# A hybrid decoder block on one core: expert stage with 2048-wide weight splits, rows out of PSUM by VectorE, pinned column transposes and slots dealt over all partitions

## The chip, the cores and the metric

The kernel runs on one core of a Trainium2 chip. Its time is the device time of one execution in microseconds; the figure given is the median of several executions. The trace is of one more execution, taken by the hardware profiler. Engines are named as in the profile: PE is TensorE (PEld its weight loads), DVE is VectorE, ACT is ScalarE, POOL is GpSimd, SP issues most DMAs.

## The reference

One block of a decoder on 1024 tokens of 2048 features, all in float32. The part that matters here is the last: a mixture of 32 experts. Every token takes the best of four groups of experts and the best two of the eight experts in it.

```python
def expert_block(args):
    xb, e = args
    a = jax.nn.silu(xb @ w_gate[e]) * (xb @ w_up[e])   # 2048 -> 512, twice
    return a @ w_down[e]                                # 512 -> 2048
...
out = zeros.at[slot_tok].add(ys * slot_gate[:, None])   # a token's two rows are summed
x = x + gt2[:, None, :] * out
return rmsnorm(x, g_final)
```

In front of it stand a pooling mixer, sparse attention with an indexer, the output projection and the router. The change leaves them as they are, but for two lines in the router's tables.

## The kernel before

**Precision.** Every float32 product is made of three matmuls in the format fp32r. `split` (L110 to L114) makes two parts of an operand: ACT casts it to `hi` (L112, `CAST`), and DVE subtracts `hi` from it to get `lo` (L112, `TENSOR_TENSOR`). `mm3` (L116 to L121) then sums hi×hi (L117), lo×hi (L120) and hi×lo (L121), in the page's names `mm<-hi,xh`, `mm<-lo,xh`, `mm<-hi,xl`.

**Slots.** The router gives every token a place in each of its two experts. An expert has 112 slots (`CAP`); slot k stands in partition k. `tables` (L1062) compares each token's place with the row `slot` (0 to 127) and sums, by matmul, a table of token numbers (`sidx`) and gates (`sgat`). Empty slots hold a number past the end, and the gather and the scatter leave them out.

**One expert.** `gather` (L1213) fetches the rows of an expert into `xg`. `columns_of` turns them: 16 transposes on PE (L1228, four to a PSUM tile `tr`), and four splits into `xh` and `xl`. `hidden` walks over the weights in chunks of 1 MB, each a raw tile of 128 x 2048: four of `w_gate`, four of `w_up`, four of `w_down`. In the text they are G0 to G3, U0 to U3 and D0 to D3. A chunk of 2048 columns stands for four steps of the contraction (or, in `w_down`, one step for four blocks of 512 output features), so 12 matmuls of 512 columns. `halves` (L1245) splits a raw tile in two pieces of 1024 columns. After U3, `sg` is gate times sigmoid times up (L1265 to L1267); it is transposed (L1271) and split into `ah` and `al`, and the down projection sums four PSUM tiles `py`. Then ACT multiplies each by the gate (L1291), POOL multiplies by the row `gt2` in place (L1292), and an indirect DMA adds the rows to the result in DRAM.

**Buffers.** There are 13 raw tiles, four pairs of `hi` and `lo` tiles of 1024 columns, two tiles `y`, four PSUM tiles `mm` and four `tr`. The six `mm` tiles of an expert (gate, up, four `py`) take the four buffers in turn, so the next expert's gate uses the buffer of the first `py`.

**Order.** A scheduler with a model of the machine sets the order of the instructions on each engine before the kernel runs; on the chip each engine keeps to its list. `last` (`keep_in_program_order`) pins an instruction behind those that were pinned before it. The split of D1 is pinned (`last if k == 1`). The loop runs over 31 experts, and the 32nd is written out behind it, with the final norm.

Of the kernel before, what the change touches and what calls it, by code (L numbers as in the profile page):

```python
# [9 lines left out]
F32 = mybir.dt.float32  # L10
# [9 lines left out]
P = 128  # L20
# [54 lines left out]
def hybrid_block(ctx, tc, x, c, w_ada, b_ada, g_mix, w_in, w_pool, pool_scale, rel_bias, w_out,  # L75
# [82 lines left out]
    # ---------------------------------------------------------------- in-projection  # L158
    keep = ctx.enter_context(ExitStack())
    with ExitStack() as es:  # L160
# [216 lines left out]
        # x * rstd * g_mix * (1 + sc1), by blocks of the contraction  # L377
# [64 lines left out]
        # sh1, by the same blocks  # L442
# [36 lines left out]
        # the pooling mixer is the same for u and for u shifted by a constant of its channel  # L479
# [20 lines left out]
        # adaLN rows gt1, sh2, sc2, gt2: products summed over k, still to be summed over partitions  # L500
# [38 lines left out]
        # threshold of the top 256 by bisection over the bits, then ties by position  # L539
        def topk(blocks, act):  # L540
# [44 lines left out]
            def settle():  # L585
                # where the count was two-sided, the bits may end one below the threshold
# [43 lines left out]
        with e1:  # L630
# [5 lines left out]
            # index key and weights  # L636
# [25 lines left out]
            # index queries and scores  # L662
# [49 lines left out]
        # queries, keys, values and the pooling mixer, in turn  # L712
        with ExitStack() as e1:
# [12 lines left out]
            # T5 bias by distance  # L726
# [93 lines left out]
    # ---------------------------------------------------------------- attention  # L820
# [122 lines left out]
    # ---------------------------------------------------------------- output projection, router  # L943
# [8 lines left out]
    with ExitStack() as es:  # L952
# [10 lines left out]
        tokn = wo.tile([P, NB], F32, name="tokn")  # L963
        nc.gpsimd.iota(slot, pattern=[[1, P]], base=0, channel_multiplier=0, allow_small_or_imprecise_dtypes=True)
        nc.gpsimd.iota(nm, pattern=[[-1, NE]], base=NE, channel_multiplier=0, allow_small_or_imprecise_dtypes=True)
# [11 lines left out]
        # h2 keeps its features, within every 512, in the order that makes a load of 512 rows of w_gate contiguous  # L977
# [82 lines left out]
        # slot of every assignment, then token and gate of every slot  # L1060
# [151 lines left out]
    # ---------------------------------------------------------------- experts  # L1212
# [9 lines left out]
    def columns_of(A, xg):  # L1222
        xh, xl = A.xh(), A.xl()
        for k4 in range(4):
            pt = tr_ps()
            for j in range(4):
                k = k4 * 4 + j
                nc.tensor.transpose(pt[:, j * P:(j + 1) * P], xg[:, k * P:(k + 1) * P], ident)  # L1228
            ks = slice(k4 * 4, k4 * 4 + 4)
            split(xh[:, ks, :], xl[:, ks, :], pt.rearrange("p (a b) -> p a b", b=P))  # L1230
        return xh, xl
# [13 lines left out]
    def halves(A, raw, pin=None):  # L1245
        out = []
# [53 lines left out]
    class Tiles:  # L1300
# [22 lines left out]
        def y(self):  # L1323
            return self.m.tile([P, D], F32, name="y", bufs=self.bufs)
# [239 lines left out]
```

## Time and profile before

| | |
|---|---|
| median of 3 executions | 2882.97 us (2879.32 to 2883.95) |
| span of the profiled execution | 2881.1 us (its first to its last instruction) |
| busy share of the span | PE 90%, PEld 72%, DVE 77%, ACT 65%, POOL 39% |
| loop of experts | about 1585 to 2805 us of the span |
| moved by DMA | 713.47 MB, 248 GB/s over the span, about 345 GB/s in the loop of experts |

A profiled execution's time isn't given beside its span; the span lies inside the range of the three timed executions, 1.9 us under their median. Busy shares are averages over stages with different limits. A matmul's row lasts some 0.39 us, but the next one may start after 0.23 us, so on PE the starts are to be read, not the durations.

### The profile page before, as it was taken

The page shows a single profiled execution, that of the slowest core. Times are in us where ns is not written, and L with a number is a line of the kernel's source. Part 1 is how long each engine was busy: PE and PEld are TensorE (multiplying, and loading weights), DVE is VectorE, ACT ScalarE, POOL GpSimd, SP SyncE. Part 2 cuts the span into 40 slices and gives each one's busy share as a digit, 9 for nine tenths or more (in the row PEclk, how much of TensorE's full clock was granted, in tenths as well). Part 3 has the DMA queues.
Part 4 walks back from the last instruction along what each step waited for, and adds up shares of the span by engine and source line. Part 5 has one row for each costly group of instructions (what it writes and reads, how often), then busy time and mean ns, then how long its engine had stood idle before and what let it go on. Part 6 is the DMA issues. An engine that isn't in the chain of part 4 may idle for free.

```text
span 2881.1 us, 37271 instructions
## 1 busy us (share of the span) xinstructions
PE 2605.7 (90%) x12032; PEld 2061.9 (72%) x12032; DVE 2207.5 (77%) x3132; ACT 1861.1 (65%) x2888; POOL 1130.3 (39%) x941
## 2 busy tenths in 40 slices
PE   5978999999988899999995999999999999999994
PEld 3666888887756577788884777777777777777773
DVE  6798888888853784334437888888888888888888
ACT  6636888787544673234234777777777777777775
POOL 2286777655774320424222332233332233332222
PEclk9999999999999999999996999999999999999996
DMA  8743555676566614644556999999999999999974
GB/s 301 267 124 115 164 154 158 190 217 186 165 190 199 193 43 128 208 151 150 168 203 253 336 353 345 350 344 335 345 346 347 359 349 346 348 359 338 344 270 168
DMA packets 301223, 713.47 MB, mean 248 GB/s; under 512 B 33196, under 2 KB 189956, under 8 KB 243236
## 3 DMA queue, kind: packets, MB, share of 16 engines
q1 hardware_dynamic: 292960, 678.04, 67.0%
q0 software_dynamic: 8064, 33.02, 5.0%
q8 instruction: 96, 1.57, 0.2%
q14 instruction: 103, 0.84, 0.1%
HBM read 655.37 MB, written 80.38 MB: 255 GB/s over the span
## 4 chain that ended last, share of the span: by engine, by line
PE 59%; DVE 15%; issue 8%; ACT 8%; DMA 7%; POOL 2%; SPq 1%; ACTq 0%; DVEq 0%; POOLq 0%
PE mm L117 16%; PE mm L120 15%; PE mm L121 15%; DMA adw<-in_w_ada_dram 4%; DVE lo L112 3%; PE tr L1228 2%; ACT y L1291 2%; POOL adacc L524 2%; ACT hi L112 2%; PE tr L120 1%; PE tr L117 1%; PE tr L121 1%; PE tr L678 1%; PE tr L677 1%; ACT adp L519 1%
## 5 line engine op out<-in xcount | busy, mean ns | idle before, releaser
L112 DVE TENSOR_TENSOR lo<-raw,hi 128x1024 fp32r<-128x1024 f32 x768 | 971.3, 1318 | 129.5 <-ACT hi L112 125.0
L112 ACT CAST hi<-raw 128x1024 fp32r<-128x1024 f32 x768 | 779.0, 1054 | 216.7 <-PE mm L121 211.1
L524 POOL TENSOR_TENSOR adacc<-adacc,adp 128x256 f32<-128x256 f32 x480 | 429.0, 894 | 198.1 <-ACT adp L519 171.4
L120 PE MATMUL mm<-lo,xh 128*128 128x512 f32 x1024 | 413.2, 404 | 42.7 <-DVE lo L112 42.5
L121 PE MATMUL mm<-hi,xl 128*128 128x512 f32 x1024 | 401.0, 392 | 0.3 <-DVE xl L112 0.3
L117 PE MATMUL mm<-hi,xh 128*128 128x512 f32 x1024 | 399.2, 391 | 0.0
L519 ACT ACTIVATE adp<-adw,cs 128x256 f32<-128x256 f32 x480 | 236.9, 505 | 154.6 <-DMA adw<-in_w_ada_dram 76.3
L1292 POOL TENSOR_TENSOR y<-y,gt 128x512 f32<-128x512 f32 x124 | 259.2, 2118 | 188.0 <-ACT y L1291 188.0
L1217 POOL DMA_INDIRECT xg<-h_d,sidx x32 | 49.1, 1534 | 666.5 <-PE tr L1228 639.8
L120 PEld LDWEIGHTS mm<-lo,xh 128*128 128x128 f32 x1024 | 192.6, 188 | 127.9 <-DVE lo L112 91.1
L120 PE MATMUL mm<-hTl,whi 128*128 128x512 f32 x544 | 216.7, 399 | 10.2 <-DVE hTl L474 9.4
L117 PEld LDWEIGHTS mm<-hi,xh 128*128 128x128 f32 x1024 | 192.8, 188 | 41.7 <-ACT xh L112 0.2
L117 PE MATMUL mm<-hTh,whi 128*128 128x512 f32 x544 | 219.1, 404 | 2.0 <-ACT whi L112 2.0
L121 PEld LDWEIGHTS mm<-hi,xl 128*128 128x128 f32 x1024 | 192.9, 188 | 37.2 <-DVE xl L112 1.1
L121 PE MATMUL mm<-hTh,wlo 128*128 128x512 f32 x544 | 214.9, 397 | 1.6 <-DVE wlo L112 1.6
L120 PE MATMUL mm<-lo,ah 128*128 128x512 f32 x512 | 200.6, 392 | 0.0
L112 DVE TENSOR_TENSOR olo<-oraw,ohi 128x1024 fp32r<-128x1024 f32 x64 | 90.8, 1421 | 136.7 <-ACT ohi L112 136.7
L121 PE MATMUL mm<-hi,al 128*128 128x512 f32 x512 | 187.3, 396 | 0.0
L684 DVE SCALAR_TENSOR_TENSOR sc<-ev,wi,sc 128x512 f32<-128x512 f32 (+2 forms) x180 | 161.1, 942 | 26.6 <-ACT ev L680 25.8
L121 PE MATMUL mm<-ohi,ml 128*128 128x512 f32 x448 | 175.7, 392 | 0.0
L117 PE MATMUL mm<-ohi,mh 128*128 128x512 f32 x448 | 175.6, 393 | 0.0
L120 PE MATMUL mm<-olo,mh 128*128 128x512 f32 x448 | 175.4, 392 | 0.0
(370 smaller groups left out, 5445.7 us busy)
## 6 DMA issues: line engine op xcount, KB each, us to landing
raw<-in_w_gate_dram SPq DMA_DIRECT2D x128, 1024.0 KB
raw<-in_w_up_dram SPq DMA_DIRECT2D x128, 1024.0 KB
raw<-in_w_down_dram SPq DMA_DIRECT2D x128, 1024.0 KB
adw<-in_w_ada_dram SPq DMA_DIRECT2D x512, 128.0 KB
wt<-in_w_ada_dram SPq DMA_DIRECT2D x64, 512.0 KB
oraw<-in_w_out_dram SPq DMA_DIRECT2D x64, 512.0 KB
wraw<-in_w_in_dram SPq DMA_DIRECT2D x60, 512.0 KB
xt<-in_x_dram SPq DMA_DIRECT2D x8, 1024.0 KB
```

What stands on the lines that cost most here:

```text
L112: for i in (nc.scalar.copy(hi, src), nc.vector.tensor_sub(lo, src, hi.bitcast(F32))):
L117: i = nc.tensor.matmul(o, a[0], b[0], start=first, stop=False)
L120: nc.tensor.matmul(o, a[0], b[1], start=False, stop=False)
L121: nc.tensor.matmul(o, a[1], b[0], start=False, stop=final)
L519: last(nc.scalar.mul(dst, adw.pop(i), cs[:, k:k + 1]))
L524: nc.gpsimd.tensor_add(acc[r, n], acc[r, n], adp.pop(i))
L677: last(nc.tensor.matmul(pd[:, :w], stk[:, tt], khs[:, c0:c0 + w], start=True, stop=False))
L684: nc.vector.scalar_tensor_tensor(sc[b][:, c0:c0 + w], rl[:, :w], wi[:, b, h:h + 1], sc[b][:, c0:c0 + w], op0=OP.mult, op1=OP.add)
L1217: nc.gpsimd.indirect_dma_start(out=xg[:CAP], out_offset=None, in_=h2_d, in_offset=bass.IndirectOffsetOnAxis(ap=idx[:CAP], axis=0), bounds_ ...
L1228: nc.tensor.transpose(pt[:, j * P:(j + 1) * P], xg[:, k * P:(k + 1) * P], ident)
L1291: nc.scalar.mul(y[:, ns], py[n4], gate)
L1292: nc.gpsimd.tensor_mul(y[:, ns], y[:, ns], gt2[:, ns])
```

## The change

Four things change in the expert stage.

1. `halves` makes one split of 2048 columns of a raw tile in place of two of 1024. There are three pairs of `hi` and `lo` tiles, each of 2048 columns, in place of four of 1024; 12 raw tiles in place of 13; and one buffer of `y` in place of two.
2. `expert` uses `gated`: one DVE instruction multiplies a PSUM tile by the gate and by `gt2` into `y`. The ACT and the POOL instruction go.
3. The transposes of the next expert's rows become a generator of four steps. Three are made ahead of the transposes of `sg` and one behind; the first transpose is pinned with `last`. The gather of the expert after the next is asked for behind the expert and no longer inside it.
4. The first 112 entries of `slot` are 0, 16, 32, ... 96, 1, 17, ...: slot k stands in partition (k mod 16)*7 + k div 16, so that the used slots of an expert lie all over the 112 partitions.

```diff
         nc.gpsimd.iota(slot, pattern=[[1, P]], base=0, ...)
+        nc.gpsimd.iota(slot[:, :CAP].rearrange("p (j i) -> p j i", i=CAP // 16), pattern=[[1, 16], [16, CAP // 16]],
+                       base=0, channel_multiplier=0, allow_small_or_imprecise_dtypes=True)
...
-    def columns_of(A, xg):
+    def columns_in_steps(A, xg, pin=None):
         xh, xl = A.xh(), A.xl()
         for k4 in range(4):
             pt = tr_ps()
             for j in range(4):
                 k = k4 * 4 + j
-                nc.tensor.transpose(pt[:, j * P:(j + 1) * P], xg[:, k * P:(k + 1) * P], ident)
+                i = nc.tensor.transpose(pt[:, j * P:(j + 1) * P], xg[:, k * P:(k + 1) * P], ident)
+                if pin and k == 0:
+                    pin(i)
             ks = slice(k4 * 4, k4 * 4 + 4)
             split(xh[:, ks, :], xl[:, ks, :], pt.rearrange("p (a b) -> p a b", b=P))
-        return xh, xl
+            yield xh, xl
...
     def halves(A, raw, pin=None):
-        out = []
-        for i in (0, 2):
-            hi, lo = A.hilo()
-            split(hi, lo, raw[:, i:i + 2, :], pin)
-            out += [(hi[:, j, :], lo[:, j, :]) for j in range(2)]
-            pin = None
-        return out
+        hi, lo = A.hilo()
+        split(hi, lo, raw, pin)
+        return [(hi[:, j, :], lo[:, j, :]) for j in range(4)]
...
-        res = nxt() if nxt else None
+
+        steps = nxt() if nxt else None
+        if steps:
+            for _ in range(3):
+                next(steps)
         pt = tr_ps()
         for k in range(4):
             nc.tensor.transpose(pt[:, k * P:(k + 1) * P], sg[:, k * P:(k + 1) * P], ident)
         ah, al = A.ah(), A.al()
         split(ah, al, pt.rearrange("p (a b) -> p a b", b=P))
-        return ah, al, wd0, res
+        return ah, al, wd0, next(steps) if steps else None
...
         for n4 in range(4):
-            ns = slice(n4 * 512, (n4 + 1) * 512)
-            nc.scalar.mul(y[:, ns], py[n4], gate)
-            nc.gpsimd.tensor_mul(y[:, ns], y[:, ns], gt2[:, ns])
+            gated(y, py[n4], gate, gt2, n4)
...
-    A.m, A.halves = m, [(mh, 2), (mh, 2), (m, 2), (m, 2)]
-    A.raws += [(m, 4)] * 4
-    early.extend(load(A, srcs.pop(0)) for _ in range(4))
+    A.m, A.halves = m, [(mh, 1), (m, 2), (m, 2)]
+    A.raws += [(m, 3)] * 3
+    early.extend(load(A, srcs.pop(0)) for _ in range(3))
...
         def nxt(e=e):
-            x_ = columns_of(A, xgs.popleft())
-            if e + 2 < NE:
-                xgs.append(gather(A, sidx[:, e + 2:e + 3]))
-            return x_
+            yield from columns_in_steps(A, xgs.popleft(), last)

         y, xe = expert(A, chunks, gt2, *xe, sgat[:, e:e + 1], nxt)
+        if e + 2 < NE:
+            xgs.append(gather(A, sidx[:, e + 2:e + 3]))
         scatter(y, sidx[:, e:e + 1])
```

What the scheduler makes of it is shown at three places of one expert in the middle of the loop.

ACT, from the sigmoid behind G3 to the first casts of the down projection, before. Two casts belong to a chunk: the four pairs behind the sigmoid are U1, U2, U3 and D0, and `hi_20429` and `hi_20433` are D1, `hi_20451` is the first half of D2.

```order
L1265 ACTIVATE sg_20364<-mm_20176 128x512
L112 CAST hi_20290<-raw_20288 128x1024
...
L112 CAST hi_20360<-raw_20354 128x1024
L112 CAST xh_20368<-tr_20370 128x512
L112 CAST xh_20368<-tr_20377 128x512
L112 CAST xh_20368<-tr_20384 128x512
L112 CAST xh_20368<-tr_20391 128x512
L112 CAST ah_20407<-tr_20402 128x512
L112 CAST hi_20429<-raw_20427 128x1024
L112 CAST hi_20433<-raw_20427 128x1024
L112 CAST hi_20451<-raw_20449 128x1024
```

The same place after. `hi_19302` is U3, `hi_19320` D0, `hi_19385` D1, `hi_19403` D2 and `hi_19421` D3.

```order
L1269 ACTIVATE sg_19324<-mm_19172 128x512
L112 CAST hi_19302<-raw_19300 128x2048
L112 CAST hi_19320<-raw_19318 128x2048
L112 CAST hi_19403<-raw_19401 128x2048
L112 CAST xh_19328<-tr_19330 128x512
L112 CAST xh_19328<-tr_19337 128x512
L112 CAST xh_19328<-tr_19344 128x512
L112 CAST ah_19356<-tr_19351 128x512
L112 CAST xh_19328<-tr_19360 128x512
L112 CAST hi_19385<-raw_19383 128x2048
L112 CAST hi_19421<-raw_19419 128x2048
```

The cast of D2 now stands ahead of the three first `xh` and of `ah`, and the cast of D1 behind the fourth `xh`. D2 takes the pair of tiles that U3 held, so its cast waits for the last matmul of the up projection.

PE, the same expert after, from the last transposes of the next rows to the first matmuls of D1 (before, the four transposes of `sg` came first, then 8 + 4 + 4 transposes of `xg`).

```order
L1231 MATMUL tr<-ident,xg 128x128 x12
L1279 MATMUL tr<-ident,sg 128x128 x4
L117 MATMUL mm<-hi,ah 128x512
L120 MATMUL mm<-lo,ah 128x512
...
L1231 MATMUL tr<-ident,xg 128x128 x4
L121 MATMUL mm<-hi,al 128x512 x4
L117 MATMUL mm<-hi,ah 128x512 x4
L120 MATMUL mm<-lo,ah 128x512
```

Twelve transposes moved ahead of those of `sg`; four stay behind the first eight matmuls of D0.

DVE, from the product with the up projection on, after. `lo_19404` is D2, `lo_19386` D1, `lo_19422` D3, `lo_19453`, `lo_19471` and `lo_19489` are G0, G1 and G2 of the next expert.

```order
L1271 TENSOR_TENSOR sg_19324<-sg_19324,mm_19245 128x512
L112 TENSOR_TENSOR lo_19404<-raw_19401,hi_19403 128x2048
...
L112 TENSOR_TENSOR xl_19329<-tr_19360,xh_19328 128x512
L112 TENSOR_TENSOR lo_19386<-raw_19383,hi_19385 128x2048
L112 TENSOR_TENSOR lo_19422<-raw_19419,hi_19421 128x2048
L112 TENSOR_TENSOR lo_19453<-raw_19450,hi_19452 128x2048
L1286 SCALAR_TENSOR_TENSOR y_19437<-mm_19367,sgat_11999,gt2_15224 128x512
L1286 SCALAR_TENSOR_TENSOR y_19437<-mm_19368,sgat_11999,gt2_15224 128x512
L112 TENSOR_TENSOR lo_19471<-raw_19468,hi_19470 128x2048
L1286 SCALAR_TENSOR_TENSOR y_19437<-mm_19369,sgat_11999,gt2_15224 128x512
L1286 SCALAR_TENSOR_TENSOR y_19437<-mm_19370,sgat_11999,gt2_15224 128x512
L112 TENSOR_TENSOR lo_19489<-raw_19486,hi_19488 128x2048
```

Four instructions that empty PSUM now stand between the subtractions of G0, G1 and G2; before, none did, and four of ACT's casts had the `y` of L1291 between them instead.

## Rows read from the trace of the kernel before

**Rows 1.** Windows: stretch, busy us (xcount) by engine, PEclk, DMA share, GB/s.
```profile
2000.00:2100.00 100.00, 92.37 (x418) 72.52 (x418) 89.58 (x84) 73.63 (x86) 26.07 (x13) 1.00 0.97 350
...
2800.00:2881.00 81.00, 42.86 (x165) 31.13 (x163) 65.11 (x104) 45.14 (x94) 18.10 (x4) 0.70 0.47 197
```
**Rows 2.** Waits, 1600 to 2750 us: us in total, times, longest.
```profile
ACT hi L112 <- DMA raw<-in_w_gate_dram: 1.2, 1, 1.2
```
**Rows 3.** Groups by form, 1600 to 2800 us: xcount, busy us, mean ns, idle before.
```profile
L112 DVE TENSOR_TENSOR lo<-raw,hi 128x1024 fp32r<-128x1024 f32 x734 | 931.1, 1322 | 120.9 <-ACT hi L112 116.7
```
**Rows 4.** Chain of waits, one expert: start us, us on the chain, what.
```profile
2060.82 0.93 PE mm L121 x4
...
2099.75 0.44 PE tr L1228 x4
2100.19 0.93 PE mm L121 x4
...
2102.49 0.23 PE mm L120
```
**Rows 5.** Timeline of PE at the end of U3: start us, us, what, idle before.
```profile
2094.22 0.39 PE L121 MATMUL mm<-hi,xl 128*128 128x512 f32 x1
2096.08 0.63 PE L1271 MATMUL tr<-ident,sg 128*128 128x128 f32 x4 [1.47 <-DVE xl L112]
2096.63 1.27 PE L1228 MATMUL tr<-ident,xg 128*128 128x128 f32 x8
2097.66 0.47 PE L117 MATMUL mm<-hi,ah 128*128 128x512 f32 x1
```
**Rows 6.** Timeline of PE in the gate projection of the same expert.
```profile
2074.31 0.39 PE L117 MATMUL mm<-hi,xh 128*128 128x512 f32 x1
...
2074.88 0.50 PE L120 MATMUL mm<-lo,xh 128*128 128x512 f32 x1 [0.18 <-DVE lo L112]
...
2076.14 0.39 PE L117 MATMUL mm<-hi,xh 128*128 128x512 f32 x1
...
2077.11 0.50 PE L120 MATMUL mm<-lo,xh 128*128 128x512 f32 x1 [0.59 <-DVE lo L112]
...
2077.45 0.40 PE L121 MATMUL mm<-hi,xl 128*128 128x512 f32 x1
...
2078.38 0.39 PE L117 MATMUL mm<-hi,xh 128*128 128x512 f32 x1
...
2079.35 0.50 PE L120 MATMUL mm<-lo,xh 128*128 128x512 f32 x1 [0.58 <-DVE lo L112]
```
**Rows 7.** Timeline of POOL in the same stretch.
```profile
2069.89 8.31 POOL L1292 TENSOR_TENSOR y<-y,gt 128x512 f32<-128x512 f32 x4 [5.38 <-ACT y L1291]
```
**Rows 8.** Timeline of DVE: three stretches of the same expert.
```profile
2074.74 2.32 DVE L112 TENSOR_TENSOR lo<-raw,hi 128x1024 fp32r<-128x1024 f32 x1
...
2076.98 2.31 DVE L112 TENSOR_TENSOR lo<-raw,hi 128x1024 fp32r<-128x1024 f32 x1
...
2098.31 2.36 DVE L112 TENSOR_TENSOR lo<-raw,hi 128x1024 fp32r<-128x1024 f32 x2
```
**Rows 9.** Timeline of ACT behind U3.
```profile
2094.42 2.05 ACT L112 CAST xh<-tr 128x512 fp32r<-128x512 f32 x4 [1.44 <-PE mm L120]
2096.74 0.59 ACT L112 CAST ah<-tr 128x512 fp32r<-128x512 f32 x1 [0.27 <-PE tr L1271]
2097.23 2.00 ACT L112 CAST hi<-raw 128x1024 fp32r<-128x1024 f32 x2
```
**Rows 10.** Groups by form, 2795 to 2881 us: the last expert and the norm.
```profile
L1522 DVE SCALAR_TENSOR_TENSOR raw<-raw,rr,xg 128x2048 f32<-128x2048 f32 x4 | 9.4, 2343 | 0.0
...
L1520 ACT ACTIVATE raw<-raw,rr 128x2048 f32<-128x2048 f32 x4 | 8.0, 1990 | 5.8 <-DVE rr L1517 5.8
...
L1278 DVE SCALAR_TENSOR_TENSOR y<-mm,sgat,gt 128x512 f32<-128x512 f32 x4 | 2.7, 744 | 1.6 <-issue 1.6
```

More of the change, by code (lines that the diff above doesn't have):

```diff
@@ L1227, in columns_of @@
                 k = k4 * 4 + j
-                nc.tensor.transpose(pt[:, j * P:(j + 1) * P], xg[:, k * P:(k + 1) * P], ident)
+                i = nc.tensor.transpose(pt[:, j * P:(j + 1) * P], xg[:, k * P:(k + 1) * P], ident)
+                if pin and k == 0:
+                    pin(i)
             ks = slice(k4 * 4, k4 * 4 + 4)
             split(xh[:, ks, :], xl[:, ks, :], pt.rearrange("p (a b) -> p a b", b=P))
-        return xh, xl
+            yield xh, xl
+    def columns_of(A, xg):
+        return list(columns_in_steps(A, xg))[-1]
     def weight_chunks(wg, wu, wd):
@@ L1323, in y @@
         def y(self):
-            return self.m.tile([P, D], F32, name="y", bufs=self.bufs)
+            return self.m.tile([P, D], F32, name="y")
         def raw(self):
@@ L1333, in hilo @@
             pool, bufs = self.halves[(self.h - 1) % len(self.halves)]
-            return [pool.tile([P, 2, 512], F32R, name=n, bufs=bufs) for n in ("hi", "lo")]
+            return [pool.tile([P, 4, 512], F32R, name=n, bufs=bufs) for n in ("hi", "lo")]
     def spread(dst, row):
@@ L1483, in hybrid_block @@
     for n4 in range(4):
-        if n4 % 2 == 0:
+        if n4 == 0:
             yh, yl = A.hilo()
         gated(y, py[n4], sgat[:, NE - 1:NE], gt2, n4)
-        ys.append((yh[:, n4 % 2, :], yl[:, n4 % 2, :]))
+        ys.append((yh[:, n4, :], yl[:, n4, :]))
         split(*ys[n4], y[:, n4 * 512:(n4 + 1) * 512])
```

## Prediction, made before the changed kernel ran

> **What bounds the kernel now.** I read the windows first. In the loop of experts PE is the busiest engine, about 92% of every 100 us, with DVE at 90% and the DMA engines at 97% [rows 1]. Three engines near the top say nothing about which one sets the pace, so the waits come next. Between 1600 and 2750 us ACT, which reads the weights first, waited for a weight DMA once, for 1.2 us [rows 2]: the transfers keep up and are not the bound, however busy their share looks. DVE stood idle 120.9 us before its subtractions, waiting for ACT's casts [rows 3]: with 734 of them at two a chunk and 24 an expert that is 30.6 experts, 4.0 us each. So DVE has room as well. What is left is PE and whatever it waits for.
>
> The chain of waits gives the period: the same four matmuls start at 2060.82 and at 2100.19 us, 39.4 us apart [rows 4]. The timeline of PE shows two places in it where PE stands still.
>
> At the end of the up projection the last matmul starts at 2094.22 and the transposes of `sg` at 2096.08 [rows 5]. A matmul hands over to the next after 0.23 us (the 0.93 us of four on the chain [rows 4]), so PE loses 1.6 us there.
>
> In the gate projection PE waits three times for a `lo`: the starts of L117 and L120 lie 0.57, 0.97 and 0.97 us apart instead of 0.23, and the matmul behind comes after 0.34 instead of 0.23 [rows 6]. That makes 0.34 + 0.74 + 0.74 + 3 x 0.11 = 2.15 us. The reason lies with POOL, which multiplies four tiles by `gt2` from 2069.89 to 2078.20 us [rows 7]. Two subtractions beside it took 2.32 and 2.31 us; two in a row without it took 2.36 together, 1.14 us from start to start [rows 8].
>
> **The change part by part.**
>
> *Rows out of PSUM by DVE.* POOL's four products go, and with them the slow subtractions: 2.15 us of PE's waits an expert lose their cause. ACT's four multiplications, which stand between its casts of the same chunks, go too; I count them in the same 2.15 us. DVE gets four instructions of the kind that the last expert already uses, 0.74 us each [rows 10]. They stand between the subtractions of G0, G1 and G2. Whether this makes PE wait again is worked out below.
>
> *Splits 2048 wide.* Twelve casts and twelve subtractions replace 24 and 24. The trace has no such cast of weights. For ACT, 2048 columns in one instruction took 1.99 us in the norm [rows 10], and two casts of 1024 in a row 2.00 us [rows 9]; both ends agree, so 2.0 us. For DVE, two starts of 1.14 us (2.28) are the lower end, 2.36 us for two in a row the upper [rows 8], and one instruction of 2048 columns with two inputs took 2.34 [rows 10]. I take 2.3 us. Throughput hardly changes; what changes is that the first matmul of a chunk needs 2.0 us of cast and the second 4.3 us of both, instead of half of that.
>
> *Transposes ahead of `sg`.* Twelve now fill the 1.6 us in which PE waited for `sg` (eight took 1.27 us [rows 5], so some 1.7 us). But ACT's list changes along with them: ahead of `ah` stand the cast of D2 and three `xh`, and behind it a fourth `xh` and only then the cast of D1. D2's cast waits for the pair of tiles that U3 holds. This is a chain of handovers, counted from the end of U3's last matmul:
>
> 1. The cast of D2 takes 2.0 us; the next instruction starts 0.1 us before its end: 1.9.
> 2. Three `xh`, 0.49 us from start to start (four end after 2.05, the last lasting 0.59 [rows 9]): 3.4.
> 3. `ah`, 0.59 us [rows 9]: 4.0. PE has long finished its sixteen transposes and stands still for 2 us.
> 4. Eight matmuls of D0 at 0.23 us: 5.8. Four transposes, 0.44 us [rows 4], and some 0.2 until they are seen: 6.4.
> 5. The fourth `xh`: 6.9.
> 6. The cast of D1, 2.0 us: 8.9.
> 7. The subtraction of D1, 2.3 us, with DVE free by then (D2's, three `xl`, `al` and one more `xl` end at about 7.7): 11.2.
>
> PE begins the lo×hi matmuls of D1 at 11.3 us. Before, the same handover took from 2094.61 (the end of the matmul that starts at 2094.22 [rows 5]) to 2102.49 us [rows 4], 7.9 us. The work of PE in between is the same. So the stretch gets 3.4 us longer: the wait for `sg` is filled, and a longer wait in three pieces takes its place, for `ah`, for the cast of D1 and for its `lo`.
>
> *G0 to G2 behind it.* From 11.3 us PE needs 1.8 us for the rest of D1 and 2.75 (12 x 0.229) for each of D2 and D3, whose parts are ready: 18.6. The cast of G0 takes the tiles of D1, free at 13.1, and ends at 15.3; its subtraction ends at 17.6. Then come two rows out of PSUM at some 0.65 us from start to start (19.0), G1's subtraction (21.3), two more rows (22.6) and G2's subtraction (25.0). PE takes G0 at 18.6, G1 at 21.35 without a wait, and reaches the lo of G2 at 24.3: it waits about 0.8 us. From there DVE needs 2.2 to 2.3 us a chunk against PE's 2.75, so it gains on PE. The lower bound is no wait at all, the upper 1.6 us (both row instructions ahead of it at their full 0.74 and the subtraction at 2.36, each handover late by 0.1).
>
> *Slots over all partitions, one raw tile less, one `y`, the later gather.* Worth nothing: weights waited 1.2 us in all [rows 2], so a more even transfer moves no wait. The cover is deep: with a chunk every 39.4 / 12 = 3.3 us, 12 raw tiles in place of 13 take 3.3 us of it. If a gather came late, PE's twelve transposes would wait where `ah` is waited for anyway. One `y` is rewritten an expert later. In the router one small POOL instruction is added.
>
> *Sum.* An expert: + 3.4 (D0 and D1) - 2.15 (POOL gone) + 0.8 (G2) = + 2.1 us, a period of 41.5 us. A check by PE's idle time: before 1.6 + 2.15 = 3.75; after 2.0 for `ah`, 0.4 for `al`, 1.3 and 1.4 for D1's two parts, 0.8 for G2, 5.9, again + 2.1. The loop has 31 of them: + 65 us. The start of the loop (the first split is whole) and the last expert may cost 1 us each: + 67. Against the profiled span of 2881.1 us that is 2948; the median of the timed runs lies 1.9 us over that span, so **2950 us**.
>
> The Trainium skill, in Perfetto Trace Analysis under Optimizing Scalar/DVE Operations, speaks against this part of the change: larger instructions help throughput where the engine is saturated, and where ScalarE or VectorE have room but cause bubbles on others, smaller ones let work go on sooner. DVE's 4.0 us of idle time an expert [rows 3] puts this kernel in the second case. By the rule's first half, were DVE saturated, the outcome would lie on the side of the first rival.
>
> **The rivals.**
>
> *Only what is removed counts (faster).* The 2.15 us of POOL and the 1.6 us at `sg` go, and nothing new is late: 39.4 - 3.75 = 35.6 us, 31 x 3.75 = 116 us less, about 2767. For it: each wait is on the profile, and the change takes away the cause of each. Against it: the order on ACT. It decides at D1's lo: if that is ready by 7.9 + 2.15 - 0.8 = 9.2 us behind U3 instead of 11.3, the kernel is no slower than before. That would need ACT to skip most of D2's cast, and it can't start that before U3 ends.
>
> *PE's clock falls as well (slower still).* The granted clock is 1.00, its level of 2.4 GHz, in the loop, and 0.70 on average in the last 81 us, where PE is busy 43% [rows 1]. After the change PE stands still some 5 us of the 11.3 behind U3, in pieces of up to 2 us, where so far the longest was 1.6. If the clock goes to 1.2 GHz there, the 6 us of PE's work in it take 12 and some 3 us of the difference are hidden in waits: + 3 us for each expert that is hit. With half of them: 2950 + 47 = 2997. The Trainium skill names the mechanism in Perfetto Trace Analysis, Matmul Optimizations: the engine scales its power with use, so matmuls should run back to back. By it this rival would hold; the trace of the loop, 1.00 throughout with waits of 1.6 us, hasn't shown it so far.
>
> *The new waits equal the old ones (no change).* That G2 doesn't wait and D1's chain is 1.3 us shorter than worked out: 2883. Nothing in the rows asks for it.
>
> **How the numbers follow.** The forecast has a chance of 83%, the clock 8%, the faster rival 6%, no change 3%. Own range of the forecast: if G2 waits for nothing and D1's chain is 0.3 us shorter than counted, + 1.0 an expert (2915); with 1.6 us for G2 and 0.3 us more on the chain, + 3.2 (2984). The lower end needs all errors on one side, so I start at 2922 and take a part of the clock's case in on top: 2922 to 2985. This kernel's measurement tells a change from none at about 0.2%, 6 us. Slower: 83 + 8 = 91%, less 1 for a small one; faster 6, same 4.
>
> **What would show it.** In the profile after: a period of some 41.5 us between the same matmuls of neighbouring experts; no row of POOL on `y`; subtractions of 2048 columns at 2.3 us and casts at 2.0; behind U3, twelve transposes, then PE idle about 2 us until `ah`, and waits for a cast and a lo of D1 of over 1 us each; one wait of under 1.6 us for a lo of G2 and none in G0, G1. It is wrong if D1's first matmul follows the fourth transposes without a wait, if the clock of the loop falls under 1.00, or if ACT waits for weight DMAs.

## The result and the profile after

| | before | after |
|---|---|---|
| median of the runs made together | 2883.46 us (2879.32 to 2884.3) | 2956.08 us (2951.37 to 2958.84) |
| ratio, with its 95% interval | 1 | 1.0256 [1.0243, 1.0269] |
| span of the profiled execution | 2881.1 us | 2949.5 us |
| profiled execution itself | not given | 2951.37 us |
| busy share of the span | PE 90%, DVE 77%, ACT 65%, POOL 39% | PE 89%, DVE 74%, ACT 59%, POOL 34% |

The changed kernel is slower by 72.6 us, and the forecast was 2950 us. The loss lies in the loop of experts. These are the transposes of `sg` of the loop's first and of its last expert, of before and then of after (durations in ns, then the starts of the first and last of the four).

```profile
L1271 PE MATMUL tr<-ident,sg x4: 273/273/302, 1585.0 to 1585.3; 128*128 128x128 f32 x4
...
L1271 PE MATMUL tr<-ident,sg x4: 272/273/327, 2804.6 to 2805.0; 128*128 128x128 f32 x4
```
```profile
L1279 PE MATMUL tr<-ident,sg x4: 272/272/273, 1578.9 to 1579.2; 128*128 128x128 f32 x4
...
L1279 PE MATMUL tr<-ident,sg x4: 272/273/333, 2871.1 to 2871.5; 128*128 128x128 f32 x4
```

Before, 31 periods took 2804.6 - 1585.0 = 1219.6 us, 39.34 each. After, they took 1292.2. That is 72.6 us more. That the medians differ by the same figure is partly chance: in the profiled executions the loop of after begins 6.1 us earlier and what follows it takes 1.9 us longer, so their spans differ by 68.4 us.

The windows of after, over the stretch shown first in [rows 1].

```profile
2000.00:2100.00 100.00, 88.57 (x383) 70.22 (x384) 79.63 (x55) 61.54 (x43) 18.38 (x5) 0.97 0.87 314
```

Every engine is less busy than in [rows 1], DMA too. ACT and POOL also lost the rows out of PSUM, but PE has the same matmuls to do: this is a loop in which more is waited for. One figure is new: the granted clock is 0.97 on average, where it was 1.00.

The groups by form, 1600 to 2800 us, as in [rows 3].

```profile
L112 DVE TENSOR_TENSOR lo<-raw,hi 128x2048 fp32r<-128x2048 f32 x347 | 786.6, 2287 | 166.2 <-ACT hi L112 158.8 <-DMA raw<-in_w_up_dram 3.8
L112 ACT CAST hi<-raw 128x2048 fp32r<-128x2048 f32 x346 | 658.9, 1913 | 376.5 <-PE mm L121 368.3 <-DMA raw<-in_w_up_dram 5.6
```

A subtraction of 2048 columns takes 2.29 us and a cast 1.91 (2.3 and 2.0 were taken). ACT stands idle 376.5 us ahead of its casts, nearly all of it until a matmul lets go of a pair of `hi` and `lo`. So ACT isn't too slow; it is let in late.

The stretch behind U3, where the prediction placed the loss. First PE's timeline after: the last matmul of U3, then the transposes and the first matmuls of D0 and D1.

```profile
2160.06 0.39 PE L121 MATMUL mm<-hi,xl 128*128 128x512 f32 x1
2160.29 1.47 PE L1231 MATMUL tr<-ident,xg 128*128 128x128 f32 x12
2161.60 0.60 PE L1279 MATMUL tr<-ident,sg 128*128 128x128 f32 x4
2164.39 0.50 PE L117 MATMUL mm<-hi,ah 128*128 128x512 f32 x1 [2.19 <-ACT ah L112]
...
2166.34 0.60 PE L1231 MATMUL tr<-ident,xg 128*128 128x128 f32 x4
2167.17 1.20 PE L121 MATMUL mm<-hi,al 128*128 128x512 f32 x4 [0.23 <-DVE al L112]
2169.42 1.20 PE L117 MATMUL mm<-hi,ah 128*128 128x512 f32 x4 [1.05 <-ACT hi L112]
2171.74 0.50 PE L120 MATMUL mm<-lo,ah 128*128 128x512 f32 x1 [1.13 <-DVE lo L112]
```

ACT in the same stretch, to be held against [rows 9]:

```profile
2160.49 1.91 ACT L112 CAST hi<-raw 128x2048 fp32r<-128x2048 f32 x1 [3.53 <-PE mm L121]
2162.30 1.55 ACT L112 CAST xh<-tr 128x512 fp32r<-128x512 f32 x3
2163.73 0.60 ACT L112 CAST ah<-tr 128x512 fp32r<-128x512 f32 x1
2166.98 0.59 ACT L112 CAST xh<-tr 128x512 fp32r<-128x512 f32 x1 [2.64 <-PE tr L1231]
2167.46 3.71 ACT L112 CAST hi<-raw 128x2048 fp32r<-128x2048 f32 x2
```

The wait of 1.47 us for `sg` [rows 5] is gone. In its place PE waits 2.19 us for `ah`, because ACT begins D2's cast only when U3's last matmul has ended (2160.45), and `ah` stands behind it. D1's cast starts at 2167.46, behind the fourth `xh`, and D1 follows with waits of 1.05 and 1.13 us. From the end of U3 to the first lo×hi matmul of D1 it is 2171.74 - 2160.45 = 11.3 us. Before, that matmul stood here in the same view:

```profile
2102.32 0.40 PE L120 MATMUL mm<-lo,ah 128*128 128x512 f32 x1
```

That is 2102.32 - 2094.61 = 7.7 us behind U3, so the stretch grew by 3.6 us.

The gate projection of the next expert: DVE, and behind it the one place where PE waits.

```profile
2175.85 2.29 DVE L112 TENSOR_TENSOR lo<-raw,hi 128x2048 fp32r<-128x2048 f32 x1 [1.96 <-ACT hi L112]
2178.06 1.40 DVE L1286 SCALAR_TENSOR_TENSOR y<-mm,sgat,gt 128x512 f32<-128x512 f32 x2
2179.38 2.28 DVE L112 TENSOR_TENSOR lo<-raw,hi 128x2048 fp32r<-128x2048 f32 x1
...
2182.90 6.68 DVE L112 TENSOR_TENSOR lo<-raw,hi 128x2048 fp32r<-128x2048 f32 x3
```
```profile
2184.59 0.39 PE L117 MATMUL mm<-hi,xh 128*128 128x512 f32 x1
2185.23 0.50 PE L120 MATMUL mm<-lo,xh 128*128 128x512 f32 x1 [0.25 <-DVE lo L112]
```

The three waits of [rows 6] are down to one, for G2, and POOL has no product on `y` any more. The starts lie 0.64 us apart where 0.23 would do, and the matmul behind starts 0.34 us later (2185.57), again for 0.23: 0.41 + 0.11 = 0.52 us.

What the prediction didn't have in its sum is PE's clock. Below is the chain of waits of after: the first matmul of D0 in three neighbouring experts, and the four transposes behind it.

```profile
2079.60 0.50 PE mm L117
...
2082.16 0.87 PE tr L1231 x4
...
2123.21 0.50 PE mm L117
...
2125.32 0.45 PE tr L1231 x4
...
2164.39 0.50 PE mm L117
```

And windows of 4 us (PE, PEld, DVE, ACT and POOL busy, then the granted clock, the DMA share and GB/s) from the first of these experts and, in the last two lines, from the second.

```profile
2076.00:2080.00 4.00, 1.81 (x15) 1.52 (x14) 2.75 (x3) 3.54 (x5) 0.00 (x0) 1.00 1.01 426
2080.00:2084.00 4.00, 4.00 (x15) 3.29 (x14) 2.65 (x5) 0.95 (x2) 0.71 (x1) 0.63 0.93 350
2084.00:2088.00 4.00, 2.05 (x7) 0.86 (x7) 2.89 (x3) 3.25 (x2) 0.30 (x1) 0.93 0.58 174
2088.00:2092.00 4.00, 4.00 (x11) 3.17 (x12) 1.96 (x1) 0.46 (x1) 0.00 (x0) 0.59 0.80 281
...
2121.00:2125.00 4.00, 1.81 (x9) 1.49 (x9) 3.75 (x4) 2.16 (x5) 0.00 (x0) 1.00 1.00 418
2125.00:2129.00 4.00, 2.72 (x13) 1.78 (x12) 2.41 (x4) 3.20 (x3) 1.01 (x1) 1.00 0.93 336
```

The two experts do the same work. In the first, the granted clock fell twice to its lower level of 1.2 GHz, after the wait for `ah` and after those for D1, and the transposes took 0.87 us instead of 0.45. The period is 43.61 us there and 41.18 in the next. Of the 31 periods six are of the long kind, 2.1 to 2.5 us longer. The loop's first period is 42.37 us, 1.2 longer, and there the clock fell once:

```profile
1582.00:1587.00 5.00, 4.75 (x16) 3.47 (x14) 3.10 (x6) 1.53 (x2) 0.98 (x1) 0.66 0.60 215
```

So the loss is 31 x (41.18 - 39.34) = 57.0 us of waits and 14.3 + 1.2 = 15.5 us in the seven experts in which the clock fell: 72.5 of 72.6.

### The profile page after: what moved, and what is told of

Read it like the earlier page. It is cut to its first block, busy times and chain, and to the rows that moved or that the text cites. A ratio compares the mean times of both kernels' runs of the same rounds, so it can differ in the third digit from the quotient of the medians.

```text
span 2949.5 us, 35968 instructions
## 1 busy us (share of the span) xinstructions
PE 2622.5 (89%) x12032; PEld 2089.4 (71%) x12032; DVE 2178.1 (74%) x2872; ACT 1745.6 (59%) x2380; POOL 1012.8 (34%) x818
## 4 chain that ended last, share of the span: by engine, by line
PE 40%; DVE 13%; ACT 10%; issue 4%; DMA 1%; SPq 1%; POOL 0%; ACTq 0%; DVEq 0%
PE mm L120 12%; PE mm L117 11%; PE mm L121 11%; DVE lo L112 7%; ACT hi L112 6%; DVE y L1286 3%; ACT xh L112 2%; PE tr L1008 1%; PE tr L120 1%; PE tr L117 1%; PE tr L888 1%; PE tr L121 1%; PE tr L1231 1%; PE tr L1001 1%; ACT ah L112 1%
## 5 line engine op out<-in xcount | busy, mean ns | idle before, releaser
L112 DVE TENSOR_TENSOR lo<-raw,hi 128x2048 fp32r<-128x2048 f32 x384 | 870.6, 2287 | 193.5 <-ACT hi L112 185.9
L112 ACT CAST hi<-raw 128x2048 fp32r<-128x2048 f32 x384 | 731.1, 1913 | 422.2 <-PE mm L121 411.1
L120 PE MATMUL mm<-lo,xh 128*128 128x512 f32 x1024 | 402.9, 394 | 7.6 <-DVE lo L112 7.6
L1302 POOL DMA_INDIRECT ya_d<-y,sidx x31 | 224.8, 7252 | 494.7 <-DVE y L1286 494.7
L117 PE MATMUL mm<-hi,ah 128*128 128x512 f32 x512 | 178.9, 410 | 100.6 <-ACT ah L112 69.0
L120 PE MATMUL mm<-lo,ah 128*128 128x512 f32 x512 | 212.9, 416 | 35.0 <-DVE lo L112 35.0
L1220 POOL DMA_INDIRECT xg<-h_d,sidx x32 | 33.9, 1059 | 565.1 <-PE tr L1231 549.7
L121 PE MATMUL mm<-hi,al 128*128 128x512 f32 x512 | 198.3, 419 | 5.4 <-DVE al L112 5.4
L117 PEld LDWEIGHTS mm<-hi,ah 128*128 128x128 f32 x512 | 95.0, 190 | 140.8 <-ACT ah L112 76.6
```

What stands on the lines that cost most here:

```text
L112: for i in (nc.scalar.copy(hi, src), nc.vector.tensor_sub(lo, src, hi.bitcast(F32))):
L117: i = nc.tensor.matmul(o, a[0], b[0], start=first, stop=False)
L120: nc.tensor.matmul(o, a[0], b[1], start=False, stop=False)
L121: nc.tensor.matmul(o, a[1], b[0], start=False, stop=final)
L1220: nc.gpsimd.indirect_dma_start(out=xg[:CAP], out_offset=None, in_=h2_d, in_offset=bass.IndirectOffsetOnAxis(ap=idx[:CAP], axis=0), bounds_ ...
L1302: nc.gpsimd.indirect_dma_start(out=ya_d, out_offset=bass.IndirectOffsetOnAxis(ap=idx[:CAP], axis=0), in_=y[:CAP], in_offset=None, compute_ ...
```

## Experiments

The theory: the loss comes from the order behind U3, where a 1.9 us cast that has to wait for U3 stands ahead of `ah`, and D1's cast behind the fourth `xh`; the waits that this makes are so long that PE's clock falls now and then. Rivals: the 2048-wide split costs by itself; VectorE's four row instructions cost; or the clock alone does it. The ratio is to runs of the kernel before on the same chip (medians of 2882.4 to 2883.9). "Loop" is the time between the first and the last transposes of `sg`, as above (before 1219.6, after 1292.2). PEclk is the granted clock of 1600 to 2700 us in one window. "Falls" is the number of the loop's 31 periods in which the granted clock was at 1.2 GHz for a time (before 0, after 7).

| run | median us | ratio to before | loop us | PEclk | falls |
|---|---|---|---|---|---|
| E1 after, columns not pinned | 2896.89 | 1.0047 [1.0029, 1.0064] | 1228.8 | 0.98 | 14 |
| E2 after, D1 not pinned | 2891.27 | 1.0029 [1.0019, 1.0039] | 1223.1 | 0.98 | 16 |
| E3 after, four wide pairs | 2862.77 | 0.9931 [0.9915, 0.9948] | 1195.5 | 0.99 | 8 |
| E4 after, PE kept busy | 2947.40 | 1.0218 [1.0201, 1.0235] | 1280.6 | 1.00 | 4 |
| E5 before, rows by DVE | 2846.78 | 0.9864 [0.9848, 0.9881] | 1182.6 | 1.00 | 1 |
| E6 before, splits 2048 wide | 2935.31 | 1.0174 [1.0157, 1.0191] | 1265.7 | 0.98 | 15 |
| E7 before, slots dealt | 2880.14 | 0.9987 [0.9977, 0.9997] | 1220.9 | 1.00 | 1 |
| E8 after, splits 1024 wide | 2864.39 | 0.9929 [0.9912, 0.9945] | 1201.9 | 0.98 | 10 |
| E9 as E8, columns not pinned | 2837.41 | 0.9843 [0.9827, 0.9859] | 1174.1 | 1.00 | 2 |
| E10 as E9, eight half pairs | 2811.17 | 0.9745 [0.9725, 0.9764] | 1144.3 | 1.00 | 0 |

**E1, the pin on the columns away.**

```diff
-            yield from columns_in_steps(A, xgs.popleft(), last)
+            yield from columns_in_steps(A, xgs.popleft())
```

> The changed kernel with one word less: the first transpose of the next columns isn't pinned, and in ACT's list the cast of D2 then stands behind ah instead of ahead of the three xh. Theory 1 (the place of D2's and D1's casts on ACT makes the chain of handovers behind U3 long): ah comes 1.8 us earlier and D1's lo with it, so the period falls from 41.2 to some 39.1 us, the wait for ah to about 0.5 us, and the clock, which fell in 6 of 31 experts, stays up: 2870 to 2890 us. Theory 2 (splits 2048 wide with three pairs of tiles starve PE in any order): no change, 2945 to 2960. Theory 3 (four more instructions on DVE are too many): no change, 2945 to 2960.

2896.89 us, 59 us less than after, and 7 over the upper end of what was expected. PE's timeline of one expert shows why most of the loss goes:

```profile
1705.30 0.66 PE L1279 MATMUL tr<-ident,sg 128*128 128x128 f32 x4 [0.78 <-DVE sg L1271]
1705.99 1.82 PE L1231 MATMUL tr<-ident,xg 128*128 128x128 f32 x12
1708.23 0.50 PE L117 MATMUL mm<-hi,ah 128*128 128x512 f32 x1 [0.41 <-ACT ah L112]
...
1713.47 0.50 PE L120 MATMUL mm<-lo,ah 128*128 128x512 f32 x1 [0.24 <-DVE lo L112]
```

The scheduler puts `sg` first again; PE waits 0.78 us there, 0.41 for `ah` (2.19 in after) and 0.24 for D1's lo (1.13). The period is 38.85 us in this stretch (the next transposes of `sg` start at 1744.15). This holds for the first 13 experts of the loop. The loop is written out expert by expert, and from the 14th on the scheduler has another order. In the 15th to the 30th PE waits in one piece for a PSUM tile that DVE has yet to empty, at the start of the next gate projection:

```profile
2189.02 0.48 PE L117 MATMUL mm<-hi,xh 128*128 128x512 f32 x1 [2.37 <-DVE y L1286]
```

There the clock falls in 13 of the 16 experts, which makes them about 40.5 us; the three others take 38.9. That is what the expected value lacked. So with D1 pinned and the splits wide, the pin on the columns is worth 59 us.

**E2, the pin on D1's split away**, the columns still pinned.

```diff
-                w = halves(A, chunks(), last if k == 1 else None)
+                w = halves(A, chunks())
```

> The changed kernel with the pin on D1's split taken away instead (the pin on the transposes stays). ACT's list then has D1's cast ahead of the xh and D2's behind ah. Theory 1: the wait for D1's cast and lo behind U3 (1.1 + 1.1 us in the profile) goes, some of the wait for ah stays: a period of 38.9 to 39.5 us, 2870 to 2895 us. Theories 2 and 3: 2945 to 2960.

2891.27 us, as expected, though the clock fell in 16 experts. With either pin alone most of the loss is gone; it takes both to make it. In most experts of the loop's second half PE's longest wait is now the one for the PSUM tile that DVE has yet to empty:

```profile
2108.76 0.47 PE L117 MATMUL mm<-hi,xh 128*128 128x512 f32 x1 [2.37 <-DVE y L1286]
```

**E3, a fourth pair of 2048 columns** in the place of two raw tiles, both pins kept.

```diff
-    A.m, A.halves = m, [(mh, 1), (m, 2), (m, 2)]
-    A.raws += [(m, 3)] * 3
+    A.m, A.halves = m, [(mh, 1), (m, 3), (m, 3), (m, 3)]
+    A.raws += [(m, 1)] * 1
...
```

> The changed kernel with four pairs of 2048 columns instead of three and ten raw tiles instead of twelve; nothing else. D2's cast then waits for U2's pair and no longer for the end of U3. Theory 1: the chain starts 2 us earlier and the waits for ah shrink: a period of 38.4 to 39 us, 2850 to 2880 us. Theory 2, taken narrowly (it is the width, not the number of pairs): over 2930. A rival on the side of DMA (weights come late once there are fewer raw tiles): ACT waits for weight DMAs and the time is over 2956.

2862.77 us, faster than before, with the wide splits and both pins in place. ACT and PE behind U3:

```profile
2443.24 0.62 ACT L112 CAST ah<-tr 128x512 fp32r<-128x512 f32 x1
...
2444.35 9.15 ACT L112 CAST hi<-raw 128x2048 fp32r<-128x2048 f32 x5
```
```profile
2448.65 0.50 PE L120 MATMUL mm<-lo,ah 128*128 128x512 f32 x1 [0.77 <-DVE lo L112]
```

Here PE waits for D1's lo alone, not for `ah` nor for D1's cast. But the order changed with the buffers: the first of the five casts is D1's (its lo starts at 2446.30), so D2's cast now stands behind `ah` and no longer ahead of it. The run shows that width and pins make no loss once there are four pairs; whether D2's cast, left in its old place, would have been free to start, it doesn't show. In the first eleven experts PE waits 2.0 us for a cast of the gate projection, and the clock falls in eight of them (40.5 us); the 20 behind take 37.4 to 37.9 without a fall. Two raw tiles less cost nothing that shows beside this.

**E4, eight more transposes of the identity** ahead of those of `sg`, whose results are overwritten.

```diff
         pt = tr_ps()
+        for k in range(8 if steps else 0):
+            nc.tensor.transpose(pt[:, k % 4 * P:(k % 4 + 1) * P], ident, ident)
```

> The changed kernel with eight transposes of the identity more an expert, ahead of those of sg and into the same PSUM tile, which the real ones then overwrite. They take 0.9 us of the 2.2 us in which PE waits for ah. Theory of the clock (it falls in 6 of 31 experts because PE stands still there, and costs 2.4 us each time): the period stays 41.2 us and no expert is longer than the others, 2938 to 2946 us. If the falls have another cause: six experts of 43.6 us as before, 2950 to 2960. If PE is what bounds this stretch: 31 x 0.9 = 28 us slower, about 2984.

```profile
2172.84 0.50 PE L117 MATMUL mm<-hi,ah 128*128 128x512 f32 x1 [1.32 <-ACT ah L112]
...
2180.18 0.50 PE L120 MATMUL mm<-lo,ah 128*128 128x512 f32 x1 [1.13 <-DVE lo L112]
```

PE does 0.87 us more work and the period stays 41.17 us, so PE's own work isn't the bound of that stretch. The loop is 11.6 us shorter than in after: the clock falls in four experts instead of seven, and costs 1.3 to 1.5 us in three of them (next to nothing in the last) instead of mostly 2.4. The median is 8.7 us lower, 1 us over the range of my theory, and its interval nearly touches that of after; in the profiled executions the loop begins 12.6 us later (1591.5 against 1578.9), which hides the gain there. In after a first fall begins 1.0 to 1.5 us behind the wait for `ah`; in E4, where that wait is shorter, none begins there, and the four that are left begin behind the waits of D1. That speaks for the waits as their cause; whether none would be left if PE were busy throughout wasn't tried.

**E5 to E7, single parts of the change put into the kernel before.** E5, the rows out of PSUM:

```diff
-            nc.scalar.mul(y[:, ns], py[n4], gate)
-            nc.gpsimd.tensor_mul(y[:, ns], y[:, ns], gt2[:, ns])
+            gated(y, py[n4], gate, gt2, n4)
```

> The kernel before, with one part of the change alone: rows leave PSUM by one VectorE instruction, so that POOL's share goes and the tile g with it; splits 1024 wide, columns not pinned, slots as before. What my theory expects: in the kernel before VectorE's instruction and POOL's stood one behind the other, so that the part alone is a gain; the period of an expert goes from 39.2 to some 38.5 us, and the time to 2855 to 2870 us (up to 2890 if the granted clock falls in some experts as it did in the run without pinned columns). The rival, that VectorE is too full to take the longer instructions: slower than before, 2895 us or more.

2846.78 us, a gain of 37 us, where 13 to 28 were expected. (The instruction that goes beside POOL's is ACT's multiplication, L1291; the expectation calls it VectorE's.) It is 1.2 us an expert where the prediction counted 2.15. The three waits of [rows 6] are gone in the expert shown; the 1.47 us for `sg` stay, and one wait is new:

```profile
2093.90 0.47 PE L117 MATMUL mm<-hi,xh 128*128 128x512 f32 x1 [0.67 <-DVE y L1278]
```

The first matmul of the gate projection takes the PSUM tile of the first `py`, and DVE empties it 0.67 us too late. In 12 of the 31 experts a wait of 0.78 us for a lo of the gate projection stands in its place.

E6, the splits 2048 wide (three pairs, eleven raw tiles):

```diff
-    A.m, A.halves = m, [(mh, 2), (mh, 2), (m, 2), (m, 2)]
-    A.raws += [(m, 4)] * 4
+    A.m, A.halves = m, [(mh, 1), (m, 2), (m, 2)]
+    A.raws += [(m, 2)] * 2
...
```

(and `halves`, the shape of the tiles and the last expert's pieces as in the change).

> The kernel before, with one part of the change alone: the splits of the weights 2048 wide (three pairs for six halves, eleven raw tiles), all else as before. My theory: the wide split as one instruction hands its columns over later, and D1's two instructions stand in a row behind U3, so this part holds the whole loss: a period of some 40.7 us against 39.2, 2925 to 2935 us without falls of the granted clock, up to 2960 with them. The rival, that the wide splits cost nothing by themselves and that only the pinned columns do: 2875 to 2890 us.

2935.31 us, 51 us more than before: the width, with the three pairs that go with it, costs by itself. But in most experts it does so in another place than the expectation named. ACT first, then PE in the gate projection:

```profile
2090.51 2.42 ACT L1287 ACTIVATE y<-mm,sgat 128x512 f32<-128x512 f32 x4 [2.21 <-PE mm L121]
2092.81 5.52 ACT L112 CAST hi<-raw 128x2048 fp32r<-128x2048 f32 x3
```
```profile
2094.79 0.51 PE L117 MATMUL mm<-hi,xh 128*128 128x512 f32 x1 [0.28 <-ACT hi L112]
2097.27 0.50 PE L120 MATMUL mm<-lo,xh 128*128 128x512 f32 x1 [1.98 <-DVE lo L112]
```

ACT's four multiplications stand ahead of the cast of G0, and PE waits for its lo 1.98 us. This is the order in 17 of the experts, and in 11 of these the clock falls as well, for 0.7 to 1.0 us each. In the first ten PE waits in small pieces instead, 0.3 us for `ah` and for `al`, 0.3 and 0.5 for two lo further on, and the period is the same 40.2 us; so ACT's rows are not the whole of the cost. The wait for `sg` stays 1.47 us in all of these. In the changed kernel ACT has no such rows, and the width's cost shows behind U3 instead.

E7, the slots:

```diff
+        nc.gpsimd.iota(slot[:, :CAP].rearrange("p (j i) -> p j i", i=CAP // 16), pattern=[[1, 16], [16, CAP // 16]],
+                       base=0, channel_multiplier=0, allow_small_or_imprecise_dtypes=True)
```

> The kernel before, with one part of the change alone: the slots dealt over all partitions. My theory: it moves work only at the start, and the time is that of before within 0.2%, 2877 to 2889 us. The rival, that the slots dealt evenly shorten the way to the first expert or the gathers: 2870 us or less.

2880.14 us, within 0.2% of before. The loop takes 1220.9 us (before 1219.6). Worth nothing, as the prediction had it.

The parts add up: rows by DVE take 37 us off (E5) and the width puts 51 on (E6), together 14; E1, the change without the pin on the columns, is 14.5 us slower than before. The pin then adds its 59 us. That is a sum of times; the waits behind them lie in different places, as the rows show.

**E8 and E9, the changed kernel with splits 1024 wide** (six half pairs of 1024), with the pin on the columns and without it.

```diff
     def halves(A, raw, pin=None):
-        hi, lo = A.hilo()
-        split(hi, lo, raw, pin)
-        return [(hi[:, j, :], lo[:, j, :]) for j in range(4)]
+        out = []
+        for i in (0, 2):
+            hi, lo = A.hilo()
+            split(hi, lo, raw[:, i:i + 2, :], pin)
+            out += [(hi[:, j, :], lo[:, j, :]) for j in range(2)]
+            pin = None
+        return out
...
-    A.m, A.halves = m, [(mh, 1), (m, 2), (m, 2)]
+    A.m, A.halves = m, [(mh, 2), (mh, 2), (m, 4), (m, 4), (m, 4), (m, 4)]
...
```

> The changed kernel with the splits back at 1024 wide (six half pairs), columns pinned, rows by one VectorE instruction, slots dealt. My theory: the width holds the loss, so that most of it goes: a period of some 39.1 us, 2875 to 2890 us without falls of the granted clock, up to 2920 with them (1.6 to 2.4 us for each expert in which it falls). The rival, that pinned columns or the rows on VectorE hold the loss: 2940 us or more.

> The changed kernel with the splits back at 1024 wide (six half pairs) and the first transpose of the columns not pinned: rows by one VectorE instruction, slots dealt, the columns in four steps remain. What it tells apart: whether the pinned columns cost by themselves or only together with the wide splits. My theory: at 1024 wide the casts that stand ahead of the one for the down projection are half as long, so the pin costs little: 2840 to 2870 us, at most 25 us less than with the pin at this width (2864), against the 59 us that the pin cost at 2048. The rival, that the pin costs the same at any width: 2805 us or less. A third, that it costs nothing at 1024: 2860 to 2870 us.

E8 took 2864.39 us and E9 2837.41, both faster than before. E8 came out 11 us under its range, E9 3 us under its own. The pin costs 27 us at 1024 columns, 2 more than the expected limit, against 59 at 2048; that it costs the same at any width, or nothing at 1024, are both out. The width costs 59.5 us without the pin (E1 against E9; some 20 of it by the clock, an estimate from the periods with and without a fall, which fell in 14 experts of E1 and in two of E9) and 92 with it (after against E8). So neither the width nor the pin holds the loss alone; together they cost 2956.08 - 2837.41 = 119 us, of which the pin alone accounts for 27 and the width alone for 59.5, and 32 come only when both are there. In E8 the waits behind U3 are 0.8 us or less in the loop's first eight experts; from the tenth to the thirtieth they are gone and the one for PSUM has become the longest:

```profile
2455.14 0.47 PE L117 MATMUL mm<-hi,xh 128*128 128x512 f32 x1 [2.59 <-DVE y L1290]
```

In E9 it is 1.44 us in the same stretch, and the clock falls in two experts instead of ten.

**E10, eight half pairs and ten raw tiles**, 1024 wide, not pinned.

```diff
-    A.m, A.halves = m, [(mh, 2), (mh, 2), (m, 4), (m, 4), (m, 4), (m, 4)]
-    A.raws += [(m, 3)] * 3
+    A.m, A.halves = m, [(mh, 2), (mh, 2)] + [(m, 6)] * 6
+    A.raws += [(m, 1)] * 1
...
```

(against E9).

> The changed kernel with splits 1024 wide, eight half pairs in place of six and ten raw tiles in place of twelve, columns not pinned. My theory: a cast waits for the pair that a matmul two chunks back holds; with as many bytes in eight half pairs as four whole pairs have, the casts run further ahead, so that PE waits less at the end of the up projection: a period of some 36.5 us, 2800 to 2815 us without falls of the granted clock, up to 2845 with them (it would be the fastest of these kernels). The rival, that ten raw tiles are too few and casts wait for weights: 2860 us or more, with waits of ACT for weight DMAs in every expert.

2811.17 us, as expected: 2.5% faster than before and the fastest of all. The window and the one wait of PE that is left between 2100 and 2122 us:

```profile
2000.00:2100.00 100.00, 96.77 (x450) 78.66 (x449) 93.91 (x97) 73.00 (x83) 9.64 (x6) 1.00 0.99 367
```
```profile
2111.46 0.66 PE L1283 MATMUL tr<-ident,sg 128*128 128x128 f32 x4 [0.78 <-DVE sg L1275]
```

PE is busy 97%, the clock 1.00, and ACT waits for no weights. Between 1600 and 2750 us ACT's casts wait 58 us in all for a pair that PE holds, where in E9 they waited 168.

## Why the prediction was right, step by step

**What bounds the kernel.** Right: PE and what it waits for. E4 adds work to PE without a cost, E10 takes waits away and gains 71 us, and E3 and E10 give up raw tiles without harm. ACT's waits for weights, one of the prediction's signs of being wrong, came to 5.6 us in all between 1600 and 2750 us (1.2 before), 0.8 at the longest.

**The chain behind U3.** Right to 0.1 us: 11.3 us worked out, 11.3 measured. Its steps, counted from 2160.45: the first `xh` behind D2's cast at 1.85 (1.9 worked out), `ah` starting at 3.3 (3.4), D0 at 3.9 (4.0), the fourth `xh` at 6.5 (6.4), D1's cast at 7.0 (6.9), D1's lo at 8.95 (8.9). Each duration came from a row of before [rows 8 to 10]. One figure beside the chain was 0.2 off: for before the prediction took the end of the stretch from the chain of waits (2102.49) and its start from the timeline; by the timeline alone it is 7.7 us, not 7.9, and the stretch grew by 3.6, not 3.4.

**G0 to G2.** The mechanism was right, the size wrong: 0.52 us instead of 0.8. By the rows of DVE above, G1's subtraction started 18.9 us behind U3 (19.0 worked out) and G2's at 22.45 (22.6): small roundings, all to one side.

**POOL gone.** The three waits of 2.15 us are gone in the changed kernel, and the sum closes: 3.6 - 2.15 + 0.52 = 1.97 us, and the period grew by 1.84. By itself the part is worth 1.2 us (E5); 0.67 or 0.78 come back as another wait. That the rows on DVE could make PE wait there, at the first matmul of the gate projection, wasn't seen; it became the longest wait of E2 and E8.

**The sum.** 65 us were forecast for the loop's waits, and they are 57. The smaller period (41.2, not 41.5) would have given about 2942. What brought the time to 2956 is the clock, the rival that was given 8%.

**PE's clock.** The forecast left the clock at 1.00, which was wrong, and a clock under 1.00 in the loop was one of the prediction's own signs that it is wrong. The rival had it fall in half of the experts at 3 us each, 47 us in all; it fell in seven of 31 at 1.2 to 2.5 us, 15.5 in all. Two errors, 8 us too much and 15.5 too little, set against each other: that the forecast is within 6 us is in part luck. The rule that the prediction cited, in the Trainium skill, Perfetto Trace Analysis, under Matmul Optimizations, is that the engine scales its power with use. The trace agrees in part: the clock is 0.63 and 0.59 in two windows above, behind waits, but it is 1.00 in the next expert with the same waits.

**Smaller instructions.** The Trainium skill, in Perfetto Trace Analysis under Optimizing Scalar/DVE Operations, says that breaking up instructions may help where an engine has room and causes bubbles on others. The runs agree: 1024 columns in place of 2048 took 92 us off after (E8). E3 shows another way out: with one more pair of buffers the kernel with wide instructions was faster than the one before.

**The first rival, that only what is removed counts**, failed where the prediction said: `ah` behind D2's cast, and D2's cast behind U3. In E3, where the fourth pair let the scheduler put D2's cast behind `ah`, PE doesn't wait for `ah`, and the kernel comes out faster than before; so does the change with 1024 columns (E8, E9).

## What to carry to other kernels

A longer instruction at the same throughput costs where it waits for a buffer: ask which release it needs, and which short instruction stands behind it in the list of its engine. Halving the instruction and having eight half pairs in the space of four whole ones, at the price of two raw tiles (E10), let ACT run ahead; a pin that costs 27 us at one width can cost 59 at twice that. And when a wait of PE in a loop grows to 2 us in one piece, keep a term for its clock beside the term for the waits. A row of one expert stands for the loop only if the order is the same in all of them: in E1, E3, E6 and E8 it wasn't.

## What the runs showed of the hardware that was not expected

The clock doesn't follow from how much PE waits in all. After waits longest behind U3, and the clock fell in seven experts; in E1, E2 and E6, which wait less, it fell in 14, 16 and 15. How the wait lies counts for more. In E1 it fell in none of the first 14 experts, in 13 of which PE waits in pieces of 0.3 to 0.8 us, and in 13 of the 16 with one wait of 2.37. In E3 it fell in eight of the eleven with one wait of 2.0 us, and in none of the other 20, with no wait over 0.9. In E8 it fell in ten of the 21 with one of 2.6, for 1.6 us each, and in none of the other ten. In these three stretches the fall began around the end of that wait, from 0.2 us before it to 1.5 behind. Behind single waits of 1.44 to 1.47 us it fell in none of before's 31 experts, of 23 in E9 and of eight in E10.

That isn't a rule yet. In E2 it fell in five of the first 13 experts, behind waits of 0.9 and 1.1 us close together, and in E4 in four, where the longest is 1.32. And in each of these runs the clock falls in some experts and not in others that have the same waits. What picks the expert stays open.

POOL's scatter takes longer where DVE writes `y`. The rows of the indirect DMA that adds `y` to the result, of before and of after:

```profile
L1296 POOL DMA_INDIRECT ya_d<-y,sidx x31 | 67.4, 2175 | 8.7 <-POOL y L1292 8.7
```
```profile
L1302 POOL DMA_INDIRECT ya_d<-y,sidx x31 | 224.8, 7252 | 494.7 <-DVE y L1286 494.7
```

2.2 us became 7.3, and in the other runs with rows by DVE it is 5.3 (E1) to 10.3 (E9); in E6 and E7, where POOL still multiplies, 3.2 and 2.2. Nothing waited for it in the stretches read, and spans on POOL are rough. No run took it apart.
